# Decoder layer on one core: the down-projection by seven products of quarter blocks, with sums of weight quarters formed in DRAM

## The chip, the core and the metric

One core of a Trainium2 chip runs the whole layer as one program. The metric is the device time of one execution in microseconds; 1420.15 us is the median of three runs before the change (1419.44 to 1420.18). Engines are named as the profile names them: PE multiplies matrices (PEld loads its stationary operand), DVE and ACT work element by element, POOL is GpSimd, SP issues transfers.

## What is computed

The layer has 1024 tokens of width 1024, in float32:

```python
h = h + mixed @ w_out[i]                       # behind short convolution and sparse attention
u = causal_dwconv(rms_norm(h, g_ffn[i]) @ w_up[i], w_ffn_conv[i])
u_gate, u_val = jnp.split(u, 2, axis=-1)
h = h + (jax.nn.silu(u_gate) * u_val) @ w_down[i]          # the down-projection: 2816 -> 1024
ple_gate = jax.nn.sigmoid(rms_norm(h, g_ple[i]) @ w_ple_gate[i])
h = h + ple_gate * (p[i] @ w_ple_proj[i])
return rms_norm(h, g_final)
```

The sparse attention takes its queries in eight blocks of 128 tokens. The change concerns the line with `w_down`, and the place where the attention's blocks end.

## The kernel before

Every large product is made of three passes, `mm3` (L184-187). Each float32 operand is split into a high part, which an ACT copy rounds (L101), and a low part, which DVE forms by a subtraction (L104); PE then multiplies high by high, high by low and low by high. One pass is a matmul of a 128x128 weight with 128x512 activations; tokens lie along the free axis.

The stages follow one another: projection in, short convolution, attention by blocks in the order 3, 7, 6, 5, 4, 2, 1, 0 (`for n, i in enumerate(seq)`, L912), out-projection, up-projection (`up`, L1125, which takes seven products of quarter blocks per output tile), down-projection (`down`, L1205), gates with the per-layer embedding (`gate`), and the final norm. Within a stage each engine runs its instructions in one order, which a scheduler lays down when the program is built; nothing is reordered on the chip.

**The end of an attention block.** `finish` (L808) adds the branches into `ya` with four POOL additions (L813). Behind them POOL copies the next blocks' masks `mk` (L706, L708), scales scores `sc`, forms `sf`, and, from the fifth block on, adds the out-projection's residual `hx` (L836).

**The up-projection's end.** Each of the 22 tiles j leaves `uc`, a page of 128x1024 that is stored to DRAM as `ad[j]`. Five DVE operations of 1024 columns (L1155, L1156, L1159) and three ACT operations make it from the convolution's inputs `xg` and `xv`.

**The down-projection.** `plan` lists the transfers of weights in the order of use; `weights(key, ahead)` sends the next ones ahead, loads into a raw page, and splits. `down(hf)` takes one half of the tokens (512 columns) through all 22 tiles j; each j has a weight page of 128x1024 and eight column chunks c, which accumulate in all eight PSUM banks:

```python
for j in range(NF - tails):
    mh, ml = act(hf, j)
    wh, wl = weights(f"down{hf}{j}", ahead=2)
    for c in range(KC):
        mm3(pd[c], wh[c], wl[c], mh, ml, j == 0, False)
```

That is 2 x 22 x 8 x 3 = 1056 matmuls, 44 weight loads of 512 KB and 44 activation loads of 256 KB. The last two or three tiles of a half are taken chunk by chunk, and behind each chunk DVE adds the result to the residual `h` (L1225), splits it with the gain, and squares are summed for the next norm.

Of the kernel before, what the change touches and what calls it, by code (L numbers as in the profile page):

```python
# [36 lines left out]
def hybrid_layer(ctx: ExitStack, tc: tile.TileContext, xT, pT, w_in, w_vg, w_out, w_up, w_down,  # L37
# [91 lines left out]
    hold = {"out00", "out10", "down00"}  # L129
# [7 lines left out]
    def fetch(upto):  # L137
        while got[0] < min(upto, len(order)) and order[got[0]] not in hold:
            key = order[got[0]]
            got[0] += 1  # L140
            src, n = src_of[key]
            if key.startswith("out"):
# [12 lines left out]
    def send(upto):  # L155
        fetch(upto)
        while sent[0] < min(upto, got[0]):
# [4 lines left out]
            if key.startswith("out1"):  # L162
                hold_out(key, raw)
                continue
            elif key.startswith("out"):
# [126 lines left out]
    for hf in range(2):  # L292
        for j in range(NF):
            plan(f"down{hf}{j}", w_down[j], D)
# [512 lines left out]

    def finish(b):  # L808
        yield from block_out(b, b.ps, b.i + 1, lambda n, g: vsw[n // 4][:, n % 4, 64 * g:64 * g + 64], "s")
        ys = scaled(b, b.py, b.cs, "s")  # L810
        for a in range(4):
            sl = slice(a * P, (a + 1) * P)
            nc.gpsimd.tensor_add(ya[a][:, b.tok], b.y[:, sl], ys[:, sl])  # L813
# [95 lines left out]

    hx, ah, al = [], [], []  # L910
    fill = conv_out()
    for n, i in enumerate(seq):  # L912
# [17 lines left out]
        merge(*gens)  # L930
        cur = nxt
# [230 lines left out]

    run = {j: up(j) for j in range(NF)}
    next(run[0])
    for j in range(NF):
# [8 lines left out]
        if j == NF - 2:  # L1174
            hold.clear()
            send(order.index("down01") + 1)
# [3 lines left out]
    hres = []  # L1180
    gh, gl, gaccs, gsteps, grb = [], [], [], [], []

    def acts_half(hf, j):
        hi, lo = halves_of(f"a{hf}{j}")
        load(f32(lo), ad[j][:, hs(hf)])
        return in_place(lo, hi)
# [8 lines left out]
    acts = {}  # L1195
    turns = [(hf, j) for hf in range(2) for j in range(NF)]

    def act(hf, j, ahead=2):
        n = turns.index((hf, j))
        for t in turns[n:n + 1 + ahead]:  # L1200
            if t not in acts:
                acts[t] = acts_half(*t)
        return acts[hf, j]

    def down(hf):  # L1205
        tok = hs(hf)
        pd = [(bank if c % 2 else sbank)(f"d{hf}{c}") for c in range(KC)]
        tails = (2, 3)[hf]
        for j in range(NF - tails):
            mh, ml = act(hf, j)  # L1210
            wh, wl = weights(f"down{hf}{j}", ahead=2)
            for c in range(KC):
                mm3(pd[c], wh[c], wl[c], mh, ml, j == 0, False)
            if hf == 0 and j >= NF - tails - KC:
                c = j - (NF - tails - KC)
                hres.append(rawpage([P, S], f"h{c}"))
                load(hres[c], hd[c])
        act(hf, NF - tails, tails + 3)
        tail = [(acts[hf, j], weights(f"down{hf}{j}", ahead=1)) for j in range(NF - tails, NF)]
        acc = page([P, 512], f"gacc{hf}")  # L1220
        for c in range(KC):
            for n, ((mh, ml), (wh, wl)) in enumerate(tail):
                mm3(pd[c], wh[c], wl[c], mh, ml, False, n == tails - 1)
            x = hres[c][:, tok]
            nc.vector.tensor_add(x, pd[c], x)  # L1225
            if hf == 0:
                gh.append(page([P, S], f"gh{c}", F32R))
                gl.append(page([P, S], f"gl{c}", F32R))
            split_gain(x, col(V_PLE + c), gh[c][:, tok], gl[c][:, tok])
            sumsq(acc, x, c == 0, f"g{hf}{c}")  # L1230
        gsteps.append(rstd_steps(grb, [acc], D, f"gn{hf}", page, columns_of(hf)))
        next(gsteps[hf])

    down(0)
    down(1)
# [19 lines left out]
    def gate(c, u):  # L1255
# [113 lines left out]
OUT2 = (P, (S - LAST) // P, D)  # L1369
NPB, NPAGE, NWR, NWT, NFP, NPW, NHALF, AHEAD = 4, 29, 2, 8, 18, 13, 8, 3  # L1370
# [122 lines left out]
```

## Time and profile before

| | |
|---|---|
| median of the runs | 1420.15 us |
| profiled execution, its own time | 1418.19 us |
| its span | 1416.4 us |
| mean granted clock of PE | 0.991 |
| from the first down-projection matmul to the first gate matmul | 1048.94 to 1309.38 us |

The page gives each engine's busy share of the span; PE has the largest by far. In the groups of instructions `d` is the accumulator of the down-projection, `down_h` and `down_l` its split weights, `a` its split activations. A matmul's mean duration of 397 ns is not its cost: matmuls are pipelined, and the next one starts 0.23 us after the one before it. The windows give busy time in a stretch, the granted clock of PE (1.00 is the upper level, 2.4 GHz) and the share of the 16 DMA engines' time.

### The profile page before, as it was taken

Reading aid. Unit: us, or ns where it says so; the run is one execution under the profiler, and the core shown is the slowest. Engines: PE = TensorE matmul, PEld = TensorE weight load, DVE = VectorE, ACT = ScalarE, POOL = GpSimd, SP = SyncE. Lnnn points to the kernel's source line nnn. Section 1 sums busy time; section 2 is a strip of 40 time slices with the busy share of each in tenths; the row PEclk is TensorE's granted clock in tenths of the full one; section 3 lists DMA queues with packets and bytes.
Section 4 is the critical chain, followed back from the end, with each engine's and each line's share of the span. In section 5 each row is a group of like instructions: output and inputs, shape, how many; then the busy total and the mean of one; then the engine's idle time right before and its main releaser. Section 6 shows DMA issues by size and latency. Waiting matters only on the chain.

```text
span 1416.4 us, 17575 instructions
## 1 busy us (share of the span) xinstructions
PE 1372.7 (97%) x6527; PEld 1082.3 (76%) x6527; DVE 928.5 (66%) x1666; ACT 627.3 (44%) x1029; POOL 131.0 (9%) x147
## 2 busy tenths in 40 slices
PE   8989999999999989899999999999999999999995
PEld 6879888866666667787888888888887888888884
DVE  7753332577778666998868767978787216524668
ACT  6233111277777644465444433544465114423543
POOL 0211011221122443000000000000000000000001
PEclk9999999999999999999999999999999999999998
DMA  7463211130012223441212222212256443532344
GB/s 270 114 183 120 92 52 38 30 90 19 12 31 65 49 81 111 157 164 60 90 65 85 87 78 75 104 63 87 82 201 223 149 130 112 203 104 83 124 135 178
DMA packets 68773, 148.64 MB, mean 105 GB/s; under 512 B 6608, under 2 KB 28112, under 8 KB 68688
## 3 DMA queue, kind: packets, MB, share of 16 engines
q1 hardware_dynamic: 68048, 144.38, 31.3%
q0 software_dynamic: 640, 3.15, 0.6%
q8 instruction: 51, 0.84, 0.3%
q14 instruction: 34, 0.28, 0.1%
HBM read 112.90 MB, written 28.31 MB: 100 GB/s over the span
## 4 chain that ended last, share of the span: by engine, by line
PE 85%; DVE 6%; DMA 3%; ACT 2%; SPq 2%; issue 1%; POOL 0%; DVEq 0%; ACTq 0%; POOLq 0%
PE d L185 6%; PE d L186 6%; PE d L187 6%; PE ua L185 4%; PE ua L186 4%; PE ua L187 4%; PE uc L186 3%; PE uc L185 3%; PE uc L187 3%; PE sy L760 2%; PE wy L760 2%; PE g L185 2%; PE g L186 2%; PE g L187 2%; PE ub L187 1%; PE ub L185 1%
## 5 line engine op out<-in xcount | busy, mean ns | idle before, releaser
L185 PE MATMUL d<-a,down_h 128*128 128x512 f32 x352 | 139.4, 397 | 2.6 <-ACT down_h L101 2.6
L186 PE MATMUL d<-a,down_h 128*128 128x512 f32 x352 | 139.5, 396 | 0.0
L187 PE MATMUL d<-a,down_l 128*128 128x512 f32 x352 | 135.8, 394 | 0.0
L104 DVE TENSOR_TENSOR down_l<-down_r,down_h 128x1024 fp32r<-128x1024 f32 x44 | 53.7, 1225 | 110.7 <-ACT down_h L101 75.7
L101 ACT ACTIVATE down_h<-down_r 128x1024 fp32r<-128x1024 f32 x44 | 46.7, 1062 | 136.2 <-DMA down_r<-in_w_down_dram 116.7
L1249 POOL DMA_DIRECT2D out_dram<-h x8 | 4.5, 564 | 843.1 <-DVE h L1248 842.8
L185 PEld LDWEIGHTS d<-a,down_h 128*128 128x128 f32 x352 | 66.7, 189 | 18.7 <-ACT down_h L101 3.1
L186 PEld LDWEIGHTS d<-a,down_h 128*128 128x128 f32 x352 | 66.6, 189 | 15.8
L187 PEld LDWEIGHTS d<-a,down_l 128*128 128x128 f32 x352 | 66.1, 188 | 15.5
L1154 ACT ACTIVATE uc<-xg,vec 128x1024 f32<-128x1024 f32 x22 | 25.4, 1154 | 92.3 <-DVE xg L1147 92.3
L101 ACT ACTIVATE in_h<-in_r 128x1024 fp32r<-128x1024 f32 (+1 forms) x20 | 20.7, 1037 | 96.4 <-PE cx L186 30.1
L1147 DVE TENSOR_TENSOR xg<-uc,e 128x512 f32<-128x512 f32 x22 | 15.2, 691 | 69.2 <-PE uc L187 69.1
L712 ACT ACTIVATE ps<-ps,stat 128x512 f32<-128x512 f32 (+7 forms) x64 | 49.2, 770 | 13.4 <-DVE stat L723 13.1
L104 DVE TENSOR_TENSOR in_l<-in_r,in_h 128x1024 fp32r<-128x1024 f32 (+2 forms) x22 | 25.0, 1140 | 28.4 <-ACT in_h L101 28.4
L185 PE MATMUL g<-gh,pg_h 128*128 128x512 f32 (+1 forms) x128 | 43.5, 340 | 0.0
L187 PE MATMUL g<-gh,pg_l 128*128 128x512 f32 (+1 forms) x128 | 43.2, 338 | 0.0
L186 PE MATMUL g<-gl,pg_h 128*128 128x512 f32 (+1 forms) x128 | 43.1, 337 | 0.0
L104 DVE TENSOR_TENSOR a<-a 128x512 fp32r<-128x512 f32 x44 | 28.6, 688 | 21.8 <-ACT a L101 21.7
L631 ACT ACTIVATE pw<-pw,stat 128x640 f32<-128x640 f32 (+3 forms) x56 | 38.3, 686 | 5.5 <-DVE stat L685 3.3
L101 ACT ACTIVATE uth<-ut 128x1024 fp32r<-128x1024 f32 x22 | 23.4, 1062 | 37.7 <-DVE ut L994 37.6
L101 ACT ACTIVATE ugh<-ugr 128x1024 fp32r<-128x1024 f32 x22 | 23.4, 1061 | 36.4 <-DMA ugr<-in_w_up_dram 36.4
L185 PE MATMUL ua<-m,uth 128*128 128x512 f32 x88 | 35.2, 400 | 3.3 <-ACT uth L101 3.3
(733 smaller groups left out, 4138.9 us busy)
## 6 DMA issues: line engine op xcount, KB each, us to landing
down_r<-in_w_down_dram SPq DMA_DIRECT2D x44, 512.0 KB, 3.7
uvr<-in_w_up_dram SPq DMA_DIRECT2D x22, 512.0 KB, 3.6
ugr<-in_w_up_dram SPq DMA_DIRECT2D x22, 512.0 KB, 4.4
ad<-uc SPq DMA_DIRECT2D x22, 512.0 KB, 2.6
a<-ad SPq DMA_DIRECT2D x44, 256.0 KB, 5.0
in_r<-in_w_in_dram SPq DMA_DIRECT2D x18, 512.0 KB, 7.1
qa<-qd SPq DMA_DIRECT2D x8, 512.0 KB, 4.7
qb<-qd SPq DMA_DIRECT2D x16, 256.0 KB, 4.7
```

The source lines that it names most:

```text
L101: nc.scalar.activation(hi, x, AF.Copy)
L104: (nc.gpsimd if (lo_eng or lo_of[0]) == "pool" else nc.vector).tensor_sub(lo, x, f32(hi))
L185: first = nc.tensor.matmul(ps, wh, mh, start=start, stop=False, **more)
L186: nc.tensor.matmul(ps, wh, ml, start=False, stop=False, **more)
L187: return first, nc.tensor.matmul(ps, wl, mh, start=False, stop=stop, **more)
L631: nc.scalar.activation(w[:, :b.nw * P], w[:, :b.nw * P], AF.Exp, bias=b.M_W[:, h:h + 1], scale=-1.0, accum_out=b.D_W[:, h:h + 1])
L712: nc.scalar.activation(w[:, :nk], w[:, :nk], AF.Exp, bias=b.M_S[:, h:h + 1], scale=-1.0, accum_out=b.D_S[:, h:h + 1])
L760: m = nc.tensor.matmul(py[64 * g:64 * g + 64, :], vals(n, g), pts[g], start=n == 0, stop=n == nblk - 1)
L1147: nc.vector.tensor_add(xg[:, hi], c, e2)
L1154: nc.scalar.activation(u, xe[:, 0:S], AF.Copy, scale=col(tap))
L1249: nc.gpsimd.dma_start(out[k], o)
```

## The change

The activations (tokens by inner width, `ad`) are cut into four quarters: b11, b12 are the first and second 512 tokens of the first eleven tiles, b21, b22 those of the last eleven. The weights are cut into four quarters, by inner half u and output half q. Seven products of sums of quarters take the place of eight products of quarters, in the order `DOWN` = 1, 2, 6, 5, 7, 3, 4. Each has 11 tiles j, four chunks c and three passes, 132 matmuls; seven make 924.

The weight operands of products 5, 6, 7 and 3 are sums, held in a DRAM buffer `wsum`. Eight transfers issued by POOL form them, four plain copies and four that add to what is there; one is issued at the end of each attention block, behind its last `ya` addition. Each is 11 tiles of 128 rows of 512 floats, 2.88 MB.

```diff
+    def down_weights():
+        a = [[w_down[u * (NF // 2):(u + 1) * (NF // 2)][:, :, hs(q)].rearrange("j p n -> p j n") for u in range(2)]
+             for q in range(2)]
+        w5, w6, w7, w3 = (wsum[q].rearrange("j p n -> p j n") for q in range(4))
+        copy, more = nc.gpsimd.dma_start, lambda d, s_: nc.gpsimd.dma_start(d, s_, accum_op=ALU.add)
+        for do, dst, src in ((copy, w5, a[1][0]), (more, w5, a[1][1]), (copy, w6, w5), (more, w6, a[0][0]),
+                             (copy, w3, w6), (more, w3, a[0][1]), (copy, w7, a[1][0]), (more, w7, a[0][0])):
+            behind(do(dst, src), pooled[0])
+            yield
...
         merge(*gens)
+        next(dsums)
```

The activation operands are formed on DVE in 22 raw pages `ar` of 128x1024, loaded once from `ad`. `operand` splits one half page for each step, and rewrites halves in place between products:

```diff
+    def operand(n, j):
+        while len(raws) < min(NF, (j if n == 1 else j + NH_ if n == 2 else NF) + 5):
+            raws.append(page([P, S], f"ar{len(raws)}"))
+            load(raws[-1], ad[len(raws) - 1])
...
+        if n == 6:
+            x = page([P, 512], f"a6{j}t")
+            v.scalar_tensor_tensor(x, b11, -1.0, b22, op0=ALU.mult, op1=ALU.subtract)
+        elif n == 7:
+            v.tensor_sub(b12, b22, b12)
+        x = x if n == 6 else {1: b11, 2: b21, 5: b11, 7: b12, 3: b22, 4: b21}[n]
+        parts = operands[n, j] = halves_of(f"a{n}_{j}")
+        split(x, *parts)
+        if n == 1:
+            v.tensor_sub(b11, b11, b12)
+        elif n == 2:
+            v.tensor_sub(b21, b21, b22)
+        elif n == 5:
+            v.tensor_sub(b21, b21, b11)
```

Weights come as 77 loads of 128x512 (256 KB) into six small buffers (`or`, `ot`), which the up-projection's temporaries also use. The main loop keeps products 1, 6 and 7 in one set of four PSUM banks, 2 in another, then 5 and 3 there, then 4 in the first; results are added to `h` and prepared for the gates as side work spread over the steps of the product that follows:

```diff
+    for n in DOWN:
...
+        for j in range(NH_ - tails):
+            prepare(prepared[0] + 1)
+            wh, wl = weights(f"down{n}_{j}", ahead=3)
+            mh, ml = operands.pop((n, j))
+            for c in range(4):
+                last[0] = mm3(ps[c], wh[c], wl[c], mh, ml, start and j == 0, j == NH_ - 1, skip_group_check=not start)[1]
+            if n in (1, 2) and j in (2, 4, 6, 8):
+                res_load(len(hres))
+            left = NH_ - tails - j
+            for _ in range(-(-len(todo) // left)):
+                todo.pop(0)()
```

The gates take the second 512 tokens first (256 columns of them in this part) and the first 512 behind them, where they took the first half first:

```diff
-            gate(c, 0)
+            gate(c, 1)
+        if c == 0:
+            gnorm(0)
             continue
         c -= 1
-        gate(c, 1)
+        if c == 0:
+            next(gsteps[0])
+        gate(c, 0)
```

What follows are rows of the order in which the program has its instructions. The line numbers of the changed kernel are its own: L191 to L193 are the three passes, L1179 to L1184 the last steps of `up`, L825 the `ya` additions, L716 and L718 the mask copies.

On PE, where the last up-projection tile has just ended and the down-projection goes on, the kernel before has the last passes over its first two tiles and the first of the third (`a_8922`):

```order
L187 MATMUL d_8913<-a_8914,down_l 128x512
L185 MATMUL d_8913<-a_8918,down_h 128x512
L186 MATMUL d_8913<-a_8918,down_h 128x512
L187 MATMUL d_8913<-a_8918,down_l 128x512
L185 MATMUL d_8906<-a_8922,down_h 128x512
L186 MATMUL d_8906<-a_8922,down_h 128x512
L185 MATMUL d_8907<-a_8922,down_h 128x512
L186 MATMUL d_8907<-a_8922,down_h 128x512
```

The changed kernel has there the low passes of its third tile and all eight high passes, then the low ones, of its fourth (`a_3`, `down_3_p`):

```order
L193 MATMUL da_8946<-a_2_8924,down_2_p 128x512
L193 MATMUL da_8947<-a_2_8924,down_2_p 128x512
L191 MATMUL da_8944<-a_3_8950,down_3_p 128x512
L192 MATMUL da_8944<-a_3_8950,down_3_p 128x512
L191 MATMUL da_8945<-a_3_8950,down_3_p 128x512
L192 MATMUL da_8945<-a_3_8950,down_3_p 128x512
L191 MATMUL da_8946<-a_3_8950,down_3_p 128x512
L192 MATMUL da_8946<-a_3_8950,down_3_p 128x512
L191 MATMUL da_8947<-a_3_8950,down_3_p 128x512
L192 MATMUL da_8947<-a_3_8950,down_3_p 128x512
L193 MATMUL da_8944<-a_3_8950,down_3_p 128x512
```

PE takes four tiles instead of two before this point, in four banks instead of eight, so it asks for `down_3_p` where it asked for the third tile's page.

On DVE before, the last operations of the final up tile stand behind one another, and the third tile's low part (the row of `down_l`) follows them:

```order
L1156 SCALAR_TENSOR_TENSOR uc_8786<-xv_8676,vec,uc_8786 128x1024
L1159 TENSOR_TENSOR uc_8786<-uc_8782,uc_8786 128x1024
L1147 TENSOR_TENSOR xg_8800<-uc_8795,e_8798 128x512
L1155 SCALAR_TENSOR_TENSOR uc_8895<-xg_8800,vec,uc_8895 128x1024
L1155 SCALAR_TENSOR_TENSOR uc_8899<-xv_8801,vec,uc_8899 128x1024
L1156 SCALAR_TENSOR_TENSOR uc_8895<-xg_8800,vec,uc_8895 128x1024
L1156 SCALAR_TENSOR_TENSOR uc_8899<-xv_8801,vec,uc_8899 128x1024
L104 TENSOR_TENSOR down_l<-down_r,down_h 128x1024
```

In the changed kernel the low part of `down_3_p` stands behind splits of `ar` pages and sums of quarters (L1207, L1212, L1214) that lie between the up tile's operations:

```order
L104 TENSOR_TENSOR a_0_9140<-ar_9042,a_0_9140 128x512
L1207 TENSOR_TENSOR ar_8910<-ar_9138,ar_8910 128x512
L104 TENSOR_TENSOR a_1_9165<-ar_9067,a_1_9165 128x512
L1212 TENSOR_TENSOR ar_9019<-ar_9019 128x512
L1207 TENSOR_TENSOR ar_8916<-ar_9163,ar_8916 128x512
L104 TENSOR_TENSOR a_2_9188<-ar_9090,a_2_9188 128x512
L1214 TENSOR_TENSOR ar_9042<-ar_9042 128x512
L1207 TENSOR_TENSOR ar_8922<-ar_9186,ar_8922 128x512
L1180 SCALAR_TENSOR_TENSOR uc_8933<-xg_8807,vec,uc_8933 128x1024
L1214 TENSOR_TENSOR ar_9067<-ar_9067 128x512
L1180 SCALAR_TENSOR_TENSOR uc_8937<-xv_8808,vec,uc_8937 128x1024
L104 TENSOR_TENSOR down_3_p<-down_3_r,down_3_p 128x512
```

From the first L1180 row at this point of the program (1352 in the order) to the row of `down_3_p` (1410) there are 59 operations: 12 of 1024 columns, 45 of 512 and two fills of two columns. Before, the same stretch of up operations holds 26 small ones fewer.

On POOL, at the end of the first attention block, the kernel before goes from the `ya` additions to the mask:

```order
L813 TENSOR_TENSOR ya_2053<-ws_2185,ss_2376 128x128
L813 TENSOR_TENSOR ya_2054<-ws_2185,ss_2376 128x128
L706 COPY mk_2389<-selb_2355 128x2x384
L708 COPY mk_2389<-wm 128x2x128
L708 COPY mk_2832<-wm 128x2x128
```

The changed kernel has the first transfer between them:

```order
L825 TENSOR_TENSOR ya_2054<-ws_2186,ss_2377 128x128
L825 TENSOR_TENSOR ya_2055<-ws_2186,ss_2377 128x128
L930 DMA wsum<-in_w_down_dram 128x11x512
L716 COPY mk_2391<-selb_2356 128x2x384
L718 COPY mk_2391<-wm 128x2x128
L718 COPY mk_2835<-wm 128x2x128
```

Seven further transfers stand likewise behind the `ya` additions of the other blocks. The second waits for the first to have landed, the third for the second, the fourth for the third, the fifth for the fourth, the sixth for the fifth and the eighth for the seventh; the seventh waits for none.

## Rows read from the trace of the kernel before

**Rows 1.** The page, sections 1 and 3: busy shares; queues with packets, MB, share.

```profile
PE 1372.7 (97%) x6527; PEld 1082.3 (76%) x6527; DVE 928.5 (66%) x1666; ACT 627.3 (44%) x1029; POOL 131.0 (9%) x147
...
q0 software_dynamic: 640, 3.15, 0.6%
```

**Rows 2.** The page, section 5: groups with busy us, mean ns, idle before.

```profile
L185 PE MATMUL d<-a,down_h 128*128 128x512 f32 x352 | 139.4, 397 | 2.6 <-ACT down_h L101 2.6
...
L1249 POOL DMA_DIRECT2D out_dram<-h x8 | 4.5, 564 | 843.1 <-DVE h L1248 842.8
...
L104 DVE TENSOR_TENSOR a<-a 128x512 fp32r<-128x512 f32 x44 | 28.6, 688 | 21.8 <-ACT a L101 21.7
```

**Rows 3.** Windows: stretch, length; PE, PEld, DVE, ACT, POOL busy; clock, DMA share, GB/s.

```profile
300.00:340.00 40.00, 39.25 (x212) 23.75 (x213) 32.09 (x107) 28.96 (x58) 9.02 (x16) 1.00 0.24 54
500.00:540.00 40.00, 35.29 (x166) 25.09 (x166) 26.85 (x73) 15.49 (x43) 16.39 (x19) 0.91 0.20 73
540.00:580.00 40.00, 35.16 (x150) 27.03 (x150) 32.26 (x46) 19.57 (x30) 9.05 (x9) 1.00 0.54 178
566.00:570.00 4.00, 2.25 (x10) 1.54 (x9) 4.00 (x8) 1.79 (x4) 0.00 (x0) 1.00 1.00 355
1040.00:1050.00 10.00, 10.00 (x45) 8.14 (x44) 10.00 (x13) 8.16 (x14) 0.00 (x0) 1.00 0.96 342
1050.00:1310.00 260.00, 257.37 (x1104) 208.01 (x1103) 119.11 (x141) 91.57 (x115) 0.00 (x0) 0.99 0.43 144
1074.00:1078.00 4.00, 4.00 (x12) 3.14 (x13) 4.00 (x5) 3.11 (x4) 0.00 (x0) 0.69 0.60 241
1078.00:1082.00 4.00, 4.00 (x17) 3.21 (x16) 2.53 (x3) 0.49 (x1) 0.00 (x0) 0.88 0.69 236
```

**Rows 4.** Timeline of PE, down-projection's ends and its stall: start, duration, operation, [idle].

```profile
1048.94 0.39 PE L185 MATMUL d<-a,down_h 128*128 128x512 f32 x1
...
1073.98 0.51 PE L185 MATMUL d<-a,down_h 128*128 128x512 f32 x1 [2.63 <-ACT down_h L101]
...
1076.29 0.63 PE L185 MATMUL d<-a,down_h 128*128 128x512 f32 x1
...
1309.38 0.39 PE L185 MATMUL g<-gh,pg_h 128*128 128x512 f32 x1
```

**Rows 5.** Timeline of DVE where the up-projection ends.

```profile
1038.08 1.28 DVE L1155 SCALAR_TENSOR_TENSOR uc<-xg,vec,uc 128x1024 f32<-128x1024 f32 x1 [0.60 <-ACT uc L1154]
1039.29 1.28 DVE L1155 SCALAR_TENSOR_TENSOR uc<-xv,vec,uc 128x1024 f32<-128x1024 f32 x1
...
1046.88 3.70 DVE L104 TENSOR_TENSOR a<-a 128x512 fp32r<-128x512 f32 x6
...
1074.11 1.28 DVE L1156 SCALAR_TENSOR_TENSOR uc<-xv,vec,uc 128x1024 f32<-128x1024 f32 x1
```

**Rows 6.** Timeline of ACT there: the copy that PE's stall waits for.

```profile
1072.87 1.06 ACT L101 ACTIVATE down_h<-down_r 128x1024 fp32r<-128x1024 f32 x1 [1.34 <-DMA down_r<-in_w_down_dram]
```

**Rows 7.** Timeline of POOL through the attention blocks.

```profile
310.59 1.70 POOL L813 TENSOR_TENSOR ya<-ws,ss 128x128 f32<-128x128 f32 x4 [2.77 <-DVE ss L788]
...
313.00 0.74 POOL L708 COPY mk<-wm 128x256 f32<-128x256 f32 x2
...
368.07 1.19 POOL L579 TENSOR_TENSOR sf<-stat,gates 128x256 f32<-128x256 f32 x2 [9.94 <-PE wy L760]
...
465.33 1.65 POOL L836 TENSOR_TENSOR hx<-ov,hx 128x512 f32<-128x512 f32 x1 [2.67 <-DVE ov L835]
...
492.60 1.28 POOL L836 TENSOR_TENSOR hx<-ov,hx 128x512 f32<-128x512 f32 x1 [0.81 <-DVE ov L835]
...
544.92 1.73 POOL L813 TENSOR_TENSOR ya<-ws,ss 128x128 f32<-128x128 f32 x4
```

**Rows 8.** Timeline of DVE behind the first block: the first reader of `mk`.

```profile
315.98 0.74 DVE L723 CUSTOM_DVE_ANT_0 ps<-s,mk,stat 128x512 f32<-128x512 f32 x1
```

**Rows 9.** Timeline of DVE behind the last gate product.

```profile
1383.72 0.42 DVE L1273 TENSOR_TENSOR h<-h,sg 128x256 f32<-128x256 f32 x1
```

More of the change, by code (lines that the diff above doesn't have):

```diff
@@ L141, in fetch @@
             src, n = src_of[key]
-            if key.startswith("out"):
+            if key.startswith("down"):
+                t, b = (("or", 2), ("ot", 4), ("ot", 4))[got[0] % 3]
+                raw = opool[0].tile([P, n], F32, tag=t, name=f"{key}_r", bufs=b)
+            elif key.startswith("out"):
                 raw = opool[0].tile([P, n], F32, tag="or", name=f"{key}_r", bufs=2)
@@ L291, in hybrid_layer @@
             plan(f"out{part}{c}", w_out[c][:, part * 512:part * 512 + 512], 512)
-    for hf in range(2):
-        for j in range(NF):
-            plan(f"down{hf}{j}", w_down[j], D)
+    wsum = dram.tile([4, NF // 2, P, 512], F32, name="wsum")
+    for n in DOWN:
+        for j in range(NF // 2):
+            if n in SUMS:
+                plan(f"down{n}_{j}", wsum[SUMS.index(n), j], 512)
+            else:
+                plan(f"down{n}_{j}", w_down[j + NF // 2 * (n != 1)][:, hs(n == 4)], 512)
     for c in range(KC):
@@ L1193, in columns_of @@
         return run
[L1195 to L1231, printed above, removed]
-        next(gsteps[hf])
@@ L1234, in hybrid_layer, with res_load, res_add, res_sq @@
-    down(0)
-    down(1)
+    def res_load(c):
+        hres.append(rawpage([P, S], f"h{c}"))
+        load(hres[c], hd[c])
+    def res_add(c, hf, ps, sign=1):
+        x = hres[c][:, hs(hf)]
+        (nc.vector.tensor_add if sign > 0 else nc.vector.tensor_sub)(x, *((x, ps) if sign < 0 else (ps, x)))
+    def res_sq(c, hf):
+        if hf not in gaccs:
+            gaccs[hf] = (page([P, 512], f"gacc{hf}"), [])
+        acc, seen = gaccs[hf]
+        sumsq(acc, hres[c][:, hs(hf)], not seen, f"g{hf}{c}")
+        seen.append(c)
@@ new lines, in res_split, with gnorm, add @@
+    def res_split(c, hf):
+        gp[c, hf] = halves_of(f"g{hf}{c}")
+        split_gain(hres[c][:, hs(hf)], col(V_PLE + c), *gp[c, hf])
+    def gnorm(hf):
+        grb[hf] = []
+        gsteps[hf] = rstd_steps(grb[hf], [gaccs[hf][0]], D, f"gn{hf}", page, columns_of(hf), lambda m: behind(m, last[0]))
+        next(gsteps[hf])
+    A = [sbank(f"da{c}") for c in range(4)]
+    side, X = [], None
+    for n in DOWN:
+        if n in (2, 5):
+            X = [bank(f"d{n}{c}") for c in range(4)]
+        if n == 4:
+            A = [sbank(f"db{c}") for c in range(4)]
+        ps = X if n in (2, 5, 3) else A
+        start = n not in (6, 7, 3)
+        tails = 3 if n == 4 else 0
+        todo = list(side)
+        for j in range(NH_ - tails):
[9 more added lines that the diff above has]
+                todo.pop(0)()
+        side = []
+        def add(f, *a):
+            side.append(lambda: f(*a))
+        for c in range(4):
+            if n == 1:
+                add(res_add, c, 0, ps[c])
+            elif n == 2:
+                add(res_add, c, 0, ps[c])
+            elif n == 6:
+                add(res_add, c, 1, ps[c])
+            elif n == 5:
+                add(res_add, 4 + c, 1, ps[c], -1)
+                add(res_sq, c, 0)
+            elif n == 7:
+                for hf in (1, 0):
+                    add(res_add, 4 + c, hf, ps[c], -1)
+            elif n == 3:
+                add(res_add, c, 1, ps[c])
+                add(res_sq, c, 1)
+                add(res_split, c, 1)
+        if n == 7:
+            for c in range(4):
+                add(res_sq, 4 + c, 1)
+                add(res_split, 4 + c, 1)
+        if n == 3:
+            add(gnorm, 1)
+            for c in range(4):
+                add(res_split, c, 0)
@@ L1236, in hybrid_layer @@
+    tail = [(operands.pop((4, j)), weights(f"down4_{j}", ahead=2)) for j in range(NH_ - tails, NH_)]
+    for c in range(4):
+        for k, ((mh, ml), (wh, wl)) in enumerate(tail):
+            last[0] = mm3(A[c], wh[c], wl[c], mh, ml, False, k == tails - 1)[1]
+        if c == 0:
+            next(gsteps[1])
+        res_add(4 + c, 0, A[c])
+        res_split(4 + c, 0)
+        res_sq(4 + c, 0)
     h = hres
```

48 lines of the change are left out of this document (34 added, 14 removed).

## The prediction

> **What bounds the kernel now.** I read the busy shares first: PE is busy for 97% of the span, DVE for 66%, ACT 44%, POOL 9% [rows 1]. An average hides stages, so the windows came next. From 1050 to 1310 us, the down-projection with the last two up tiles in it, PE is busy 257.37 of 260 us, DVE 119.11, ACT 91.57, and the DMA engines 0.43 of their time [rows 3]. That stage is bound by PE, at the upper clock level but for one place. The groups show 352 matmuls for each of the three passes and only 2.6 us of PE idle before them [rows 2], and the timeline finds all of it at one instruction: at 1073.98 PE waits 2.63 us for a weight's high part [rows 4], which ACT copies at 1072.87, after the transfer [rows 6]. So in this stage removed matmuls are removed time, as long as DVE, ACT and the transfers keep pace. The chain of waits agrees: its largest entries are passes of `d`.
>
> Two other places are of another kind. From 500 to 580 us PE is busy only 35 of each 40 us [rows 3], so a delay on POOL or of a transfer can show there at once. From 1040 to 1050 us DVE is busy 10.00 of 10 and the DMA engines 0.96 at 342 GB/s, while PE still runs without a gap [rows 3]: at this transition nothing is spare but PE's lead.
>
> **Matmuls removed.** 1056 become 924: 132 fewer, of the same 128x512 shape. What one costs: between the first `d` at 1048.94 and the first gate matmul at 1309.38 [rows 4] lie 1056 + 48 matmuls (48 belong to the last up tiles; the window counts 1104 [rows 3]). Of the 260.44 us, 2.63 are the stall. The clock stood at the lower level behind it: a granted 0.69 and 0.88 in two windows of 4 us [rows 3] make (0.31 + 0.12) x 2 x 4 = 3.4 us there, with matmuls of 0.63 us [rows 4], and half of that, 1.7 us, is lost. Some 0.4 us is other gaps. (260.44 - 2.63 - 1.7 - 0.4) / 1104 = 0.2316 us. 132 x 0.2316 = **-30.6 us**.
>
> **Can DVE and ACT keep pace afterwards?** A step is now 12 matmuls, 2.78 us. DVE splits an activation half and a weight page and forms about one sum: three 512-wide operations. Six such in a row take 3.70 us [rows 5], so 0.61 each, 1.83 us a step. Side work adds 4 to 16 operations per 11 steps, 0.2 to 0.9 us a step. That is 2.0 to 2.7 of 2.78 us: it fits, with the fullest product close to the limit and a lead of three steps before it. ACT does about half of that count. One weight load of 256 KB per step is 94 GB/s, against 342 reached [rows 3]. I take 0, and up to +3 for the fullest product.
>
> **The transition from up to down.** Here the change moves work to the worst place. In the changed order DVE has 59 operations from the first L1180 to the low part of `down_3_p`. At 1.21 us for each of 12 wide ones (spacing of the row at 1038.08, 1.28 long, to the next) and 0.61 for 45 narrow ones that is 42 us. Started at 1038.08 as now [rows 5], it ends near 1080. Before, the same chain ends with the wide operation at 1074.11 and waits in between. PE, counted from 1048.94 at 0.2316 each, reaches `down_3_p` (row 4748 of the order, 84 matmuls on) at 1068.4. Step by step:
> - the last up tile's third product waits for DVE's L1168 (row 1388) to free its bank: DVE reaches it about 1.35 us after PE;
> - the first high pass with `down_3_p` waits for an ACT copy that now stands behind two copies of the up tile (1.06 us each, as the copy in [rows 6]), which wait for DVE's row 1398 near 1071.4: the high part is there at about 1074.2, so PE waits 4.35;
> - the eight high passes last to 1076.0 and the low part is there at 1080: 3.9.
>
> Together 9.6 instead of 2.63 us, with one stretch at the lower clock in both: **+7**. If the scheduler's order runs with fewer waits than I count, DVE's 26 extra operations cost nothing and the stall stays or goes (0, or -2.6); if the page loads, 18 of 512 KB and 7 of 256 KB, 34 us at 342 GB/s, come late on top or the clock falls twice, +13.
>
> **Eight transfers issued by POOL.** The trace shows POOL's own issue only for a 384 KB store of 128 rows: 0.56 us [rows 2]. The new ones have 11 x 128 rows. The lower end is 0.56 us each, the upper 11 times it, 6.2 us; I take the upper end's size, since the rows are what differs. Who waits: behind the first stands the mask, copied until 313.7 [rows 7] and first read at 315.98 [rows 8], so 2.3 us of slack against 6.2 in a stretch where PE is busy 39.25 of 40 [rows 3]: up to 3.9 us late. Behind the next three POOL was idle about 10 us before its next operation, as at 368.07 (9.94, the least of the three) [rows 7]: hidden. Behind the fifth to seventh stands `hx` with 2.67, 0.81 and less slack [rows 7], in the part where PE has gaps of its own. Of the 3.9 and about 12 us late, most falls on waits that other work covers. I take **+3**, ends 0 and +8.
>
> **Their traffic.** A copy carries 2.88 MB, 8.4 us of all engines at 342 GB/s; an accumulating one reads twice, so 17 us, 25 if reads and writes are carried apart. Issued behind the eight `ya` groups from 310.59 to 544.92 [rows 7], 33.5 us apart on the mean, they run where the engines are busy 0.20 to 0.24 [rows 3], and no wait of one for the one before it should last. The Trainium skill agrees on the direction (Collectives: The Full Stack, "The bandwidth ceiling: the fold count and why AG ≠ RS ≠ AR"): the in-line add costs no cycles of its own but a second source read. No row here shows an accumulating transfer.
> The eighth is different: issued near 547, behind the additions at 544.92 [rows 7], it runs into 550 to 575, where the out-projection's and up-projection's weights load; at 566 to 570 the engines are full (1.00, 355 GB/s) and PE is busy 2.25 of 4 us [rows 3]. 17 us of engine time into some 25 that are over half taken should push something: **+3**, ends 0 (from 540 to 580 the engines are busy 0.54, so there are gaps to find [rows 3]) and +10.
>
> **The tail.** The last gate product is now 512 wide, so three DVE operations behind it last 0.69 instead of 0.42 us [rows 2, 9]; a wait for a transfer covered part: **+0.5**, ends 0 and +1.
>
> **Sum.** -30.6 + 7 + 3 + 3 + 0.5 = -17.1. The profiled execution took 1418.2 us (span 1416.4 and 1.8 around it), so 1401.1; the median of the runs lay 2.0 above the profiled one: **1403 us**.
>
> **Rivals.**
> 1. *All of the additions are covered.* The transition stalls as before, POOL's issue is short, the traffic finds gaps. -30.6 + 0.5 = -30: 1390 us. For it: DMA idle shares and POOL's 9%; against it: DVE at 10.00 of 10 in the window at 1040.
> 2. *Half is lost.* The transition costs 13 and either POOL's issue 8 or the eighth transfer 10, the rest as above: -30.6 + 13 + 8 + 3 + 0.5 = -6, 1414 us.
> 3. *Slower: POOL stands still behind an accumulating transfer.* The third transfer waits in POOL's order for the second, the fifth for the fourth, and masks and scores stand behind them. The blocks' ends leave 33.5 us on the mean for each; with slack of 10 and about 3 us behind, a duration T costs (T - 43.5) + (T - 36.5), which eats the 17 us gained from T = 49 us on. At T = 60 it is 40: 1443 us. For it: nothing here shows such a transfer, and 2 KB rows are small. Against it: the software queue's packets carried 3.15 MB in 0.6% of 16 engines' span [rows 1], 23 GB/s per engine, as the hardware queue does at its fullest (342 / 16 / 0.96 = 22); T would have to be three times my 17.
> A rule that would feed the same stall: the Trainium skill says that GpSimd writes the descriptors of its transfers into SBUF and is shut out while DVE holds their shared port (DMA: Bandwidth & Descriptors, "SWDGE vs HWDGE vs iDMA"). DVE is busy 32.09 of 40 us in these stretches [rows 3]; by that rule the issue could last several times 6 us, and its chance is in rival 3.
> That the change does not do what it says can be left out: the order has 924 matmuls.
>
> **How the numbers follow.** Forecast (a gain of 9 to 24 us, 1396 to 1411): 0.58. Rival 1: 0.17. Rival 2: 0.11. Rival 3 and its like: 0.09. What is left, 0.05, lies at no change. A measurement of this kernel can tell 0.2%, 2.8 us, from no change; so faster 0.86, same 0.05, slower 0.09. The range takes the forecast, rival 2 and most of rival 1, and leaves out the slower cases: 1389 to 1418.
>
> **What would show it.** Right: 924 matmuls of `da`, `db` and the X banks at 0.23 us; PE idle of 7 to 12 us between about 1060 and 1085 with DVE full; masks behind the first transfer up to 4 us late; a fuller DMA share at 546 to 575 with longer PE waits for `out_p`. Wrong: PE waits for DVE in the steady products (then DVE is the bound), a POOL row with waits of tens of microseconds behind a `wsum` transfer (rival 3), or no stall at the transition (rival 1).

## The result, and the profile after

The changed kernel takes 1409.43 us, the median of four runs (1407.03 to 1412.71), against 1420.16 us before on the same chip: a ratio of 0.9927 with a 95% interval of 0.9903 to 0.9951. It is faster by 10.7 us; 17 were forecast. The time lies in the stated range. The profiled execution took 1407.71 us (span 1405.8), 10.5 less than that of before. So the sign and the mechanism held, two terms of the sum were too small, and one was too large.

Four points at which both programs have come equally far divide the span: the first `ya` addition on POOL, `an0s` (the small matmul of the attention's last norm), the first up-projection matmul `ua` and the first gate matmul `g`. Their starts are from the views by tile; every kernel of this study is in the table, in us.

| kernel | to first `ya` | `ya` to `an0s` | `an0s` to `ua` | `ua` to `g` | `g` to end | span |
|---|---|---|---|---|---|---|
| before | 310.6 | 246.5 | 67.6 | 684.7 | 107.0 | 1416.4 |
| after | 311.5 | 246.9 | 73.7 | 666.9 | 106.8 | 1405.8 |
| e1, two transfers earlier | 312.3 | 247.4 | 68.6 | 666.5 | 107.1 | 1401.8 |
| e2, order pinned | 312.7 | 247.1 | 75.5 | 666.0 | 106.7 | 1408.0 |
| e3, sums later | 311.6 | 247.3 | 76.1 | 659.5 | 106.6 | 1401.1 |
| e4, pages loaded by POOL | 312.1 | 246.2 | 73.5 | 660.4 | 106.6 | 1398.8 |
| e5, no transfers | 310.1 | 246.7 | 67.3 | 663.8 | 106.6 | 1394.5 |
| e6, e3 and e4 | 310.8 | 246.7 | 75.7 | 654.7 | 106.5 | 1394.4 |
| e7, e1, e3 and e4 | 311.0 | 247.2 | 69.1 | 653.9 | 106.6 | 1387.8 |
| e8, e3 and e4, no transfers | 311.8 | 246.2 | 67.4 | 653.3 | 106.6 | 1385.3 |

Each row of the table is one profiled execution. e1 to e4 ran on one chip and e5 to e8 on another; the kernel before took 1419.72 us on the first and 1418.61 us on the second (medians), and each ratio below is to before on the same chip. The first column lies ahead of everything that was changed; it moves by 2.6 us from run to run, so a difference of that size between two spans needs a look at where it is. After against before: +0.9 there, +0.4 in the attention blocks, **+6.1** from the attention's end to the up-projection, **-17.8** from there to the gates, -0.2 at the tail.

The page of after, in the lines that answer to [rows 1, 2]: PE's busy time, the software queue, and two groups of down-projection matmuls.

```profile
PE 1349.2 (96%) x6395; PEld 1061.7 (76%) x6395; DVE 990.3 (70%) x1803; ACT 643.0 (46%) x1095; POOL 141.7 (10%) x155
...
q0 software_dynamic: 9216, 26.22, 7.6%
...
L191 PE MATMUL da<-a,down_p 128*128 128x512 f32 x132 | 54.2, 411 | 7.7 <-ACT down_p L101 7.7
...
L193 PE MATMUL da<-a,down_p 128*128 128x512 f32 x132 | 51.3, 404 | 3.1 <-DVE down_p L104 3.1
```

PE's busy time fell by 23.5 us, not by 30: part of what was removed came back as slower matmuls, with a mean granted clock of 0.983 where it was 0.991. The idle time before `da` is 7.7 and 3.1 us, where the one group of before had 2.6 [rows 2]. The software queue went from 0.6% to 7.6% of the engines' span. The windows, to be held against [rows 3], columns as there:

```profile
300.00:340.00 40.00, 39.07 (x212) 23.13 (x211) 32.41 (x107) 28.93 (x58) 10.00 (x16) 1.00 0.47 131
550.00:560.00 10.00, 8.58 (x38) 6.60 (x36) 7.73 (x12) 3.45 (x5) 1.44 (x2) 1.00 1.06 217
560.00:570.00 10.00, 4.59 (x11) 3.34 (x12) 8.39 (x12) 3.46 (x6) 2.24 (x2) 0.56 1.10 236
1068.00:1072.00 4.00, 1.35 (x6) 0.75 (x4) 4.00 (x6) 0.18 (x1) 0.00 (x0) 1.00 0.82 274
1088.00:1092.00 4.00, 0.85 (x2) 0.50 (x2) 4.00 (x6) 0.63 (x1) 0.00 (x0) 0.50 0.67 272
1104.00:1300.00 196.00, 196.00 (x850) 158.55 (x849) 139.30 (x220) 96.45 (x166) 0.00 (x0) 1.00 0.35 113
```

Between 300 and 340 us the DMA engines' share doubled, and PE's busy time is that of before within 0.2 us. From 550 to 570 the DMA engines are busy all the time (the share can exceed 1, as a packet counts whole in the window in which it starts), and from 560 to 570 PE is busy 4.59 of 10 us at a granted clock of 0.56. Before had, in that window:

```profile
560.00:570.00 10.00, 7.65 (x32) 5.59 (x31) 9.88 (x17) 5.84 (x11) 0.00 (x0) 1.00 0.92 299
```

So the engines are fuller in time than before and yet carry fewer bytes, 236 GB/s instead of 299. Then 1068 to 1092, with PE idle again and the clock down to 0.50, the lower level. From 1104 to 1300 PE has no gap at all: the steady products are bound by PE, as the forecast had it, with DVE at 139.30 of 196 in this stretch.

The timeline of PE after, its long waits:

```profile
565.41 0.79 PE L191 MATMUL oa<-yan,out_p 128*128 128x512 f32 x1 [6.69 <-DVE yan L104]
...
1073.72 0.79 PE L191 MATMUL da<-a,down_p 128*128 128x512 f32 x1 [4.37 <-ACT down_p L101]
...
1085.63 0.50 PE L191 MATMUL da<-a,down_p 128*128 128x512 f32 x1 [3.32 <-ACT down_p L101]
...
1091.49 2.07 PE L193 MATMUL da<-a,down_p 128*128 128x512 f32 x4 [3.15 <-DVE down_p L104]
```

At the first of these matmuls PE had waited 0.62 us before:

```profile
558.52 0.50 PE L185 MATMUL oa<-yan,out_p 128*128 128x512 f32 x1 [0.62 <-ACT out_p L101]
```

So there is one long wait at the out-projection that did not exist before, and three at the transition where [rows 4] has one: 4.37 + 3.32 + 3.15 = 10.84 us.

POOL after, at the first, second and sixth transfer, against [rows 7]:

```profile
311.50 1.70 POOL L825 TENSOR_TENSOR ya<-ws,ss 128x128 f32<-128x128 f32 x4 [2.78 <-DVE ss L798]
313.13 1.23 POOL L930 DMA_DIRECT2D wsum<-in_w_down_dram  x1
314.36 0.85 POOL L716 COPY mk<-selb 128x768 f32<-128x768 f32 x1
...
358.61 1.92 POOL L927 DMA_DIRECT2D wsum<-in_w_down_dram  x1
...
368.95 1.18 POOL L589 TENSOR_TENSOR sf<-stat,gates 128x256 f32<-128x256 f32 x2 [8.01 <-PE wy L770]
...
492.59 1.85 POOL L927 DMA_DIRECT2D wsum<-in_w_down_dram  x1
```

An issue lasts 1.1 us for a copy and 1.9 for an accumulating transfer, not 6. The second transfer waits for the first to have landed, but that had landed some 33 us before, and POOL went on without a wait. The views by line of the accumulating transfers (L927), and below them of the copies (L930), give their time to landing:

```profile
L927 POOL DMA_DIRECT2D wsum<-in_w_down_dram x4: 1851/1868/1919, 358.6 to 547.6; - x4
...
DMA to landing us min/median/max: 18.3/19.6/23.8
```

```profile
DMA to landing us min/median/max: 11.2/12.1/12.9
```

Some 12 us for a copy and 20 for an accumulation, against gaps of 33.5 us on the mean; rival 3 needed 49.

### The profile page after: what moved, and what is told of

Its sections match the earlier page's. It is cut to its first block, busy times and chain, and to the rows that moved or that the text cites. A ratio compares the mean times of both kernels' runs of the same rounds, so it can differ in the third digit from the quotient of the medians.

```text
span 1405.8 us, 17553 instructions
## 1 busy us (share of the span) xinstructions
PE 1349.2 (96%) x6395; PEld 1061.7 (76%) x6395; DVE 990.3 (70%) x1803; ACT 643.0 (46%) x1095; POOL 141.7 (10%) x155
## 4 chain that ended last, share of the span: by engine, by line
PE 88%; DVE 6%; DMA 2%; SPq 1%; issue 1%; ACT 1%; POOL 0%; DVEq 0%; ACTq 0%; POOLq 0%
PE ua L193 4%; PE ua L191 4%; PE ua L192 4%; PE uc L191 3%; PE uc L193 3%; PE uc L192 3%; PE sy L770 2%; PE da L191 2%; PE d L193 2%; PE d L191 2%; PE d L192 2%; PE da L192 2%; PE wy L770 2%; PE da L193 2%; PE g L191 2%; PE g L192 2%
## 5 line engine op out<-in xcount | busy, mean ns | idle before, releaser
L101 ACT ACTIVATE down_p<-down_r 128x512 fp32r<-128x512 f32 x77 | 47.8, 626 | 72.8 <-PE da L193 26.1
L104 DVE TENSOR_TENSOR down_p<-down_r,down_p 128x512 fp32r<-128x512 f32 x77 | 52.4, 687 | 29.3 <-ACT down_p L101 29.2
L1179 ACT ACTIVATE uc<-xg,vec 128x1024 f32<-128x1024 f32 x22 | 25.3, 1151 | 97.0 <-DVE xg L1172 97.0
L1172 DVE TENSOR_TENSOR xg<-uc,e 128x512 f32<-128x512 f32 x22 | 15.2, 691 | 74.3 <-PE uc L193 74.1
L191 PE MATMUL da<-a,down_p 128*128 128x512 f32 x132 | 54.2, 411 | 7.7 <-ACT down_p L101 7.7
L101 ACT ACTIVATE a<-ar 128x512 fp32r<-128x512 f32 x66 | 40.5, 624 | 35.1 <-PE d L193 16.0
L104 DVE TENSOR_TENSOR a<-ar,a 128x512 fp32r<-128x512 f32 x66 | 44.5, 686 | 14.7 <-ACT a L101 14.5
L722 ACT ACTIVATE ps<-ps,stat 128x512 f32<-128x512 f32 (+7 forms) x64 | 49.1, 770 | 12.4 <-DVE stat L733 12.1
L193 PE MATMUL da<-a,down_p 128*128 128x512 f32 x132 | 51.3, 404 | 3.1 <-DVE down_p L104 3.1
L192 PE MATMUL da<-a,down_p 128*128 128x512 f32 x132 | 54.2, 410 | 0.0
L193 PE MATMUL d<-a,down_p 128*128 128x512 f32 x132 | 52.1, 395 | 0.0
L191 PE MATMUL d<-a,down_p 128*128 128x512 f32 x132 | 52.1, 395 | 0.0
L192 PE MATMUL d<-a,down_p 128*128 128x512 f32 x132 | 52.0, 394 | 0.0
L191 PE MATMUL g<-g,pg_h 128*128 128x256 f32 (+1 forms) x128 | 43.5, 339 | 0.0
L192 PE MATMUL g<-g,pg_h 128*128 128x256 f32 (+1 forms) x128 | 43.2, 338 | 0.0
L193 PE MATMUL g<-g,pg_l 128*128 128x256 f32 (+1 forms) x128 | 43.1, 338 | 0.0
```

Source lines behind the costliest of these rows:

```text
L101: nc.scalar.activation(hi, x, AF.Copy)
L104: (nc.gpsimd if (lo_eng or lo_of[0]) == "pool" else nc.vector).tensor_sub(lo, x, f32(hi))
L191: first = nc.tensor.matmul(ps, wh, mh, start=start, stop=False, **more)
L192: nc.tensor.matmul(ps, wh, ml, start=False, stop=False, **more)
L193: return first, nc.tensor.matmul(ps, wl, mh, start=False, stop=stop, **more)
L722: nc.scalar.activation(w[:, :nk], w[:, :nk], AF.Exp, bias=b.M_S[:, h:h + 1], scale=-1.0, accum_out=b.D_S[:, h:h + 1])
```

## Experiments

Two theories stood for the 6.1 us behind the attention. In the changed order two ACT copies of `out_p` stand behind three copies of `yan`, which wait for the norm; before, they stand ahead of it. Either that order costs (A), or the eighth transfer's traffic makes the weights `out_r` late whatever the order (B).

**e1: the last two transfers earlier.**

```diff
-        for do, dst, src in (... (copy, w7, a[1][0]), (more, w7, a[0][0])):      # one per block
+        for block in (((copy, w5, ..), (copy, w7, ..)), ((more, w5, ..), (more, w7, ..)),
+                      ((copy, w6, w5),), ((more, w6, ..),), ((copy, w3, w6),), ((more, w3, ..),)):
```

> The changed kernel, with the two transfers of product 7 issued at the first two blocks beside those of product 5, so that the last accumulating transfer goes out six blocks in (near 491 us) and none runs into the out-projection. Theory (the place of the eighth transfer costs what the stretch from 545 us to the first down-projection matmul lost, 6.8 us): PE's wait of 6.69 us before out_p falls under 2.5, the first da matmul comes near 1050 instead of 1056.6, and the time is about 1402.5 us. Rival (the transfers cost by their traffic wherever they run, or by POOL's issue): the loss moves with them and the time stays within 2 us of 1409.

Measured: 1403.96 us (1403.44 to 1405.23), ratio to before 0.9895 (0.9881 to 0.9909). PE's waits in the out-projection:

```profile
560.97 0.50 PE L191 MATMUL oa<-yan,out_p 128*128 128x512 f32 x1 [0.56 <-ACT out_p L101]
...
572.22 0.50 PE L193 MATMUL oa<-yan,out_p 128*128 128x512 f32 x1 [1.75 <-DVE out_p L104]
```

Before had 0.62 and 1.75 us at the same matmuls; the wait of 6.69 is gone. `an0s` to `ua` fell from 73.7 to 68.6 us; 67.6 is what it was. The first `da` matmul, which I had named as a sign, came at 1057.7, not near 1050: this order starts `da` at another place among the up matmuls, so it was a bad mark, and the table's are used instead. What follows: the place of the transfers costs 5 of the 6.1 us. The edit moves the seventh as well as the eighth, but the seventh, issued at 527.08 in the changed kernel, had landed 12.9 us later, ahead of the out-projection. In this kernel the scheduler also lays the `out_p` copies ahead of the `yan` copies again, so A and B both survive this run.

**e2: the order of before with the transfers of after.**

```diff
+            if hf == 0:
+                behind(high, held[3][0])      # yan's copy on ACT behind out_p's second copy
+                behind(mul, held[3][1])       # the norm's multiplication on DVE behind out_p's second low part
```

> The changed kernel with its eight transfers where they are, but two copies of out_p on ACT and their low parts on DVE held ahead of the norm's copies (yan), as the kernel before has them; the changed kernel's order has them behind three yan copies. Theory A (the scheduler's order is what costs): PE's wait of 6.69 falls under 3 us, time about 1404 to 1405. Theory B (the eighth transfer fills the DMA engines and out_r lands late whatever the order): PE waits as long, now for a transfer, and the time stays at 1407 to 1411.

Measured: 1406.95 us (1406.40 to 1409.79), ratio 0.9917 (0.9903 to 0.9930). PE's two longest waits up to 570 us:

```profile
561.95 0.50 PE L193 MATMUL oa<-yan,out_p 128*128 128x512 f32 x1 [1.83 <-ACT out_p L101]
...
565.14 0.79 PE L193 MATMUL oa<-yan,out_p 128*128 128x512 f32 x1 [2.46 <-ACT out_p L101]
```

The view of waits from 545 to 600 us (who for whom: us in total, times, longest), of before, of after and of e2:

```profile
ACT out_p L101 <- DMA out_r<-in_w_out_dram: 1.4, 1, 1.4
ACT out_p L101 <- DMA out_r<-in_w_out_dram: 5.5, 1, 5.5
ACT out_p L101 <- DMA out_r<-in_w_out_dram: 6.4, 2, 3.8
```

PE's single wait is now several, 7.9 us in all, and behind them ACT waits 6.4 us for `out_r` to land. The longest landing of an `out_r` from 530 to 600 us is 7.4 us after and 7.1 in e2, where the eighth transfer runs beside it, against 4.5 before and 3.5 in e1. `an0s` to `ua` is 75.5 us, no better than 73.7. Theory A falls for this stretch; B stands: with the engines full, the weights are late, and the order of the copies only chooses which wait shows. The median is 2.5 us lower, just under the 1407 that B named, but the intervals of the two ratios overlap, and the stretch that the edit touches did not gain.

**e3: the sums of activations held back.** At the transition, the second and third wait were forecast from DVE's queue.

```diff
-        split(x, *parts)
-        if n == 1:
-            v.tensor_sub(b11, b11, b12)
+        lows[n, j] = split(x, *parts)[1]
+        if n == 2:
+            behind(v.tensor_sub(b11, b11, b12), lows[n, j])
...                                                    # likewise 2 -> 6, 5 -> 7, and 7 behind lows[5, j]
```

> The changed kernel, with the sums of activation quarters on DVE (products 1, 2, 7 and 5) held behind the splits of the next product but one, so that they leave the transition: 19 operations fewer stand ahead of the low part of down_3. Theory (DVE's queue makes the waits of 3.32 and 3.15 us at down_3): both fall under 1 us, the wait of 4.37 at down_2 stays, the lower clock gets shorter, and the time falls by 6 to 10 us, to about 1401. Rival (the page and weight transfers are what is late): the waits stay, the time moves by less than 2 us.

Measured: 1402.85 us (1398.28 to 1403.22), ratio 0.9878 (0.9862 to 0.9895).

```profile
1077.58 0.73 PE L191 MATMUL da<-a,down_p 128*128 128x512 f32 x1 [4.44 <-ACT down_p L101]
...
1087.60 0.50 PE L191 MATMUL da<-a,down_p 128*128 128x512 f32 x1 [1.23 <-ACT down_p L101]
```

The wait of 4.37 (here 4.44) stays, that of 3.32 is 1.23, that of 3.15 is gone; the first of these two stays a little above the 1 us that was expected. The time at the lower clock, summed over windows of 4 us from 1040 to 1120 as in the forecast, fell from 13.6 us to 3.4, the value of before. `ua` to `g` gained 7.4 us: 5.2 of idle time, and the rest in the clock.

**e4: page loads issued by POOL.** The first wait stood in no step of the forecast. SP and ACT after show it:

```profile
1055.45 12.39 SPq L1199 DMA_DIRECT2D ar<-ad  x6
1067.94 0.85 SPq L155 DMA_DIRECT2D down_r<-in_w_down_dram  x2
```

```profile
1073.04 0.63 ACT L101 ACTIVATE down_p<-down_r 128x512 fp32r<-128x512 f32 x1 [4.86 <-DMA down_r<-in_w_down_dram]
...
1082.88 1.13 ACT L1179 ACTIVATE uc<-xg,vec 128x1024 f32<-128x1024 f32 x1
...
1084.96 2.70 ACT L101 ACTIVATE down_p<-down_r 128x512 fp32r<-128x512 f32 x5
```

ACT waits 4.86 us for `down_r`, which SP issued at 1067.94, behind six loads of `ar` that SP took 12.39 us to issue, since pages for them come free only with PE's last up matmuls. The second wait is the chain of the forecast: the two copies of the up tile, at 1082.88 and 1083.92, and `down_3`'s high part behind them. The third ends with the low part that DVE forms behind the up tile's operations:

```profile
1089.55 1.28 DVE L1180 SCALAR_TENSOR_TENSOR uc<-xv,vec,uc 128x1024 f32<-128x1024 f32 x1
1090.74 1.29 DVE L104 TENSOR_TENSOR down_p<-down_r,down_p 128x512 fp32r<-128x512 f32 x2
```

```diff
-            load(raws[-1], ad[len(raws) - 1])
+            nc.gpsimd.dma_start(raws[-1], ad[len(raws) - 1])
```

> The changed kernel, with the 22 loads of activation pages issued by POOL instead of SP, so that weight loads no longer stand behind loads that wait for pages. Theory (down_2's weight was issued at 1067.94 because six page loads stood ahead of it on SP): it is issued before 1062, the wait of 4.37 us goes, time about 1404. Rival (the buffer it goes into, shared with the up-projection's temporaries, is not free before): it is issued as late as now, the wait stays, time within 2 us of 1409.

Measured: 1402.18 us (1400.84 to 1404.33), ratio 0.9883 (0.9869 to 0.9896). SP, and PE's waits:

```profile
1053.16 22.07 SPq L155 DMA_DIRECT2D down_r<-in_w_down_dram  x5
```

```profile
1071.94 0.50 PE L191 MATMUL uc<-m,ush 128*128 128x512 f32 x1 [1.46 <-DVE xv L1168]
...
1081.82 0.50 PE L191 MATMUL da<-a,down_p 128*128 128x512 f32 x1 [4.04 <-ACT down_p L101]
...
1087.49 1.19 PE L193 MATMUL da<-a,down_p 128*128 128x512 f32 x4 [2.37 <-DVE down_p L104]
```

No page load stands between the weight loads any more, but the row of five from 1053.16 on has waits inside it. The load that went out at 1067.94 goes out at 1064.55, not before 1062 as expected: SP waits 10.9 us until DVE's L1172 has read a temporary of the up-projection, with which the weights share their buffers (the view of SP's waits, and SP from 1064 on):

```profile
SPq L155 <- DVE xg L1172: 10.9, 1, 10.9
```

```profile
1064.55 1.73 SPq L155 DMA_DIRECT2D down_r<-in_w_down_dram  x2
```

The page loads' waits now stand on POOL, one of them for a matmul of the last up tile:

```profile
1065.89 0.53 POOL L1199 DMA_DIRECT2D ar<-ad  x1 [5.29 <-PE ua L193]
```

And the wait at `down_2` is gone. So theory and rival each hold in part: the buffer sets the time to 1064.55, and the page loads added the 3.4 us behind it, which were enough to make PE wait. In its place PE waits 1.46 us for DVE's L1168, the very wait that the forecast had put first, at 1.35 us; in the changed kernel no wait shows there. The waits at `down_3` stay, 4.04 and 2.37, as they should.

**e5: no transfers.** `next(dsums)` is taken out, and products 5, 6, 7 and 3 read plain quarters of the weights, straight from `w_down` instead of `wsum`; the sums are missing from what it computes.

> The changed kernel without the eight transfers: products 5, 6, 7 and 3 read plain quarters of the weights instead of sums, so the sums are left out of the result. Theory (what the transfers cost is one thing, the traffic of the eighth): the stretch from the attention's last norm matmul to the first up matmul shrinks from 73.6 to about 67.6 us, as before, and the time is that of the early issue less 1 us or equal to it, 1402.5 to 1404. Rival (six transfers under the attention blocks cost too): more than 3 us below the early issue, under 1401.

Measured: 1398.17 us (1396.60 to 1399.18), ratio 0.9854 (0.9840 to 0.9867): lower than expected, and 5.8 us under e1, which ran on the other chip. By the table, `an0s` to `ua` is 67.3, as forecast; the attention blocks, under which seven transfers had run, take 246.7 against 246.9. The larger part against e1 lies where no transfer runs: 2.2 us ahead of the first block, and 2.7 us from `ua` to `g`, with 10.2 instead of 13.6 us at the lower clock. So the median came where the rival had put it, but the profile doesn't show the cost in the stretch that the rival named; how much of the 5.8 us between the two medians the transfers make stays open here. e7 against e8, on one chip, is the cleaner pair.

**e6 and e7: the edits together.**

> The changed kernel with both edits of the transition: sums held back on DVE, and page loads issued by POOL. Theory (two separate queues, DVE's and SP's, make the three waits): all waits of down matmuls together come under 3 us (from 10.8), first up matmul to first gate matmul about 656 us (666.9, with either edit alone 660), time about 1398. Rival (both edits relieve the same thing): no better than either alone, about 1402.

Measured for e6: 1396.13 us (1395.16 to 1396.55), ratio 0.9839 (0.9826 to 0.9853). Two waits of 1.22 us are left, and no window of 4 us from 1040 to 1120 is at the lower clock; `ua` to `g` is 654.7. Either edit alone gave 659.5 and 660.4: the gains, 7.4 and 6.5, give 12.2 together, most of their sum. So they are two queues, DVE's and SP's.

> The changed kernel with early issue, sums held back and page loads on POOL. If the three causes are separate, their gains add: 5 us for the early issue, 7.4 for the sums, and what the page loads add, so 1393 to 1397; the full saving of the matmuls alone would be 1389. If they overlap, 1398 to 1401.

Measured for e7: **1389.60 us** (1387.95 to 1391.96), ratio 0.9796 (0.9782 to 0.9810). That is below the 1393 to 1397 that was expected, and at the 1390 that rival 1 of the prediction gave for additions that are all covered. The gains of e1, e3 and e4 in the medians, 5.5, 6.6 and 7.3 us, add to 19.3, and the median is 19.8 below that of after, so as far as these numbers tell the three causes are separate. Its windows at the out-projection, and its one wait at the transition:

```profile
550.00:560.00 10.00, 9.48 (x42) 7.22 (x41) 7.29 (x11) 2.83 (x5) 2.99 (x2) 1.00 0.45 135
560.00:570.00 10.00, 8.50 (x36) 6.25 (x34) 9.67 (x17) 6.01 (x11) 0.00 (x0) 1.00 0.82 292
```

```profile
1066.65 0.50 PE L191 MATMUL uc<-m,ush 128*128 128x512 f32 x1 [1.47 <-DVE xv L1169]
```

From 560 to 570 PE is busy 8.50 us instead of 4.59, at the full clock. This version is 29.0 us faster than before on its chip. The changed kernel ran on the other chip; by the two ratios, 0.9796 and 0.9927, e7 is 1.3% faster than it, some 19 us.

**e8: e7's edits of the transition, without the transfers** (plain quarters again).

> As the run before with all three edits, but without the transfers (plain quarters of weights in place of sums, so the sums are left out of the result). Tells what the transfers cost at the best place found: if they are hidden under the attention blocks, within 1.5 us of the run with all three; if not, 2 to 5 us faster.

Measured: 1387.57 us (1386.94 to 1388.18), ratio 0.9780 (0.9766 to 0.9793). 2.0 us under e7, though the intervals of the two ratios overlap. The profiled executions are 2.5 us apart: 1.0 in the attention blocks, 1.7 between `an0s` and `ua`, 0.6 from there to the gates, and 0.8 the other way ahead of everything that was changed. So at the best place tried the transfers may still cost about 2 us; that is not clear of the noise, and why the stretch behind `an0s` gained, with the last transfer of e7 issued at 492.51, stays open.

## Why the prediction was right, and where its sizes were off

- **Matmuls removed, -30.6 us: right.** In e7, with 1.47 us of waits at the transition, `ua` to `g` is 30.8 us shorter than before. PE's busy time in that stretch fell from 678.77 to 648.89 us, 29.9, and its idle time by the rest. The clock has no share in it: in windows of 10 us both have 6.8 us at the lower level there (0.83 and 0.83 in two of before, 0.68 and 0.98 in two of e7). So about 30 us are the matmuls'.
- **The steady products fit on DVE: right.** PE is busy 196.00 of 196 us from 1104 to 1300.
- **The transition, +7 us: too small, it was 12.8** (30.6 less 17.8). The forecast had three waits of 9.6 us in all, and 10.84 came, but not the same ones. Those for the high and low part of `down_3`, 4.35 and 3.9 by the order's bookkeeping, were 3.32 and 3.15, and e3 shows that DVE's queue makes 2.1 of the first and all of the second. The wait at `down_2`, 4.37, was missed: the step counted DVE and ACT and left out the queue of SP, where the weight load waits for its buffer and then behind the page loads (e4). That the total of the waits came so near is luck. And "one stretch at the lower clock in both" was wrong: three waits that ended within 18 us of each other left PE 13.6 us at the lower level instead of 3.4. 8.2 us of waits more leave 4.6 of the 12.8 for slower matmuls, and the clock can make up to (13.6 - 3.4) / 2 = 5.1. The upper end of this step, +13, was set for page loads that come late or a clock that falls twice, so the cause stood in the forecast as its bad case.
- **POOL's issue, +3 us: too large, it was 0.4 at most,** which the spread of that stretch, 246.2 to 247.4 us over the ten kernels, does not tell from nothing. I had taken the end proportional to rows, 6.2 us; 1.1 and 1.9 were measured, nearer to the 0.56 of the only row there was. The mask copies behind the first transfer ended at 315.89 instead of 313.74, not 4 us late, and nothing waited. The Trainium skill (DMA: Bandwidth & Descriptors, "SWDGE vs HWDGE vs iDMA") has DVE lock GpSimd out of the descriptor rings while DVE runs in its 2-port mode, and the forecast had taken any busy DVE for that. With DVE busy 32.41 of 40 us no issue of the changed kernel took more than 1.92 us; the profile does not show DVE's mode, so no run here tests the rule itself.
- **The eighth transfer, +3 us: too small, it was about 6**, and e1 gives 5 of it back, e5 all. The place, the cause and the upper bound of 10 were right. The size was taken as the engine time that must be pushed aside; it is the wait of the first weights that PE needs, and what the clock loses behind it: the first 13 matmuls from the end of the wait of 6.69 on last 0.63 us or more, where 0.39 is usual.
- **Landing times: right in kind.** 18.3 to 23.8 us for an accumulation against 11.2 to 12.9 for a copy. The medians, 19.6 and 12.1, are in a ratio of 1.6. The Trainium skill's account of ReduceScatter (Collectives: The Full Stack, "The bandwidth ceiling: the fold count and why AG ≠ RS ≠ AR"), in which the add costs a second source read and no cycles of its own, agrees in direction; no run here shows what the longer time is made of.
- **The tail, +0.5 us: it was -0.2,** which is nothing.
- **Small slips.** The page loads of the transition's bad case are 33 us at 342 GB/s, not 34. Behind the seventh block POOL's slack was 1.63 us, more than the 0.81 behind the sixth. The 0.4 us of other gaps between matmuls is in no row: of the 260 us, the 2.63 that PE was not busy are the stall. None of the three moves the sum.

The sum with the measured terms: +0.9 + 0.4 + 6.1 - 17.8 - 0.2 = -10.6 us of span. From the -17.1 of the forecast it is +5.8 (transition) + 3.1 (eighth transfer) - 2.6 (issue) - 0.7 (tail) + 0.9 (ahead of all that was changed). It was luck that the issue's term, 2.6 too large, made up for part of the 8.9 that the two others were short.

## What to carry to other kernels

When a change saves work on the engine that bounds a stage, look for the gain at the stage's entrance: there the other engines still finish the stage before, and every in-order queue, the one that issues transfers included, must be walked row by row. A big transfer costs little while the DMA engines are mostly idle (about 2 us for all eight in e7 against e8, not clear of the noise), and much where the next stage's first weights load: with the last two issued at the first two blocks, 5 us came back. Waits of several microseconds can cost more than their length: behind the three of 4.37, 3.32 and 3.15 us PE was at the lower clock for 13.6 us in all, behind the one of 2.63 before for 3.4, and behind the two of 1.22 in e6 for none.

## What the runs showed of the hardware

An addition of 512 columns on DVE, 0.69 us elsewhere, lasted 2.94 us while POOL issued the eighth transfer and added behind it (DVE, then POOL, after):

```profile
548.37 2.94 DVE L225 TENSOR_TENSOR aacc<-aacc,ya01sq 128x512 f32<-128x512 f32 x1
551.41 0.69 DVE L225 TENSOR_TENSOR aacc<-aacc,ya02sq 128x512 f32<-128x512 f32 x1
```

```profile
547.56 1.87 POOL L927 DMA_DIRECT2D wsum<-in_w_down_dram  x1
548.68 2.07 POOL L848 TENSOR_TENSOR hx<-ov,hx 128x512 f32<-128x512 f32 x1
```

In the kernel before, the same addition took 1.79 us, beside POOL's `hx` alone, which lasted 1.68 us instead of 2.07. It is no accident of one execution: the addition took 2.94 to 2.97 us in the five kernels that issue the eighth transfer there (after, e2, e3, e4, e6), and 1.79 in the five that do not (before, e1, e5, e7, e8). So the issue of a transfer lengthens what DVE and POOL do beside it; by what mechanism, the profile does not show.

Two transfers issued side by side land later. In e7, where each of the first two blocks issues two, the longest copy took 20.5 us to land and the longest accumulation 32.0, against 12.9 and 23.8 in the changed kernel, which issues them one by one.
